# A diffusion block with two token mixers on one core: scan state carried by four 128x64 matmuls, inversion list in 64x64 tiles, order tables set anew

## The chip, the cores and the metric

The kernel runs on one core of a Trainium2 chip. The metric is the device time of one execution in microseconds (us). Five engines each work through a fixed list of instructions: TensorE (PE, its weight loads shown apart as PEld), VectorE (DVE), ScalarE (ACT), GpSimd (POOL) and SyncE (SP, which issues most of the DMA transfers). Each waits, through semaphores, for what the others produce.

## The reference

One layer is computed for 256 latent tokens, with 256 context tokens ahead of them as a prefix, all in fp32, with a width of 2048. Cut to what matters here:

```python
mod = silu(c) @ w_ada + b_ada                     # six shifts, scales and gates; the context has its own
h, hc = modulate(rmsnorm(x), ...), modulate(rmsnorm(ctx), ...)
rw, cv, z, ab, gt = split(h @ w_in)               # one projection feeds both mixers; gt are the merge gates
# mixer A, RWKV-7: 16 heads of 64, two directions, context first, then latent
s = s * w_t - (s @ kk_t) b_t + v_t k_t            # state, token by token;  y_t = s @ r_t
# mixer B, gated DeltaNet: 8 heads of 128, two directions, chunks of 64 tokens
u, wk = solve(I + strict_lower(kb kc^T * decay), [v*beta, kb*exp(gc)])
v_new = u - wk @ s;  o = q_dec @ s + qk @ v_new;  s = s * g_last + k_tail^T @ v_new
y = (sigmoid(g_a) * (o_a @ p_a) + sigmoid(g_b) * (o_b @ p_b)) @ w_out
x = x + gt1 * y
x = x + gt2 * swiglu(modulate(rmsnorm(x), ...))   # hidden width 5632
return rmsnorm(x, final_norm_w)
```

## The kernel before

**The products.** Each fp32 weight is split into a high and a low part (`whi` by an ACT cast, `wlo` by a DVE subtraction), the features likewise (`hxh`, `hxl`). A product is then three matmuls for each of the 16 k tiles: whi with hxh, whi with hxl, wlo with hxh. Matmuls between plain fp32 operands, which the mixers use, go to the chip as two instruction pairs (a weight load and a matmul each), so that one such matmul in the code is two matmul records in the trace and four instructions.

**Stages.** The modulation and the low-rank projections come first, up to about 200 us. Then comes the part that the change touches, which we call the weave, up to about 1310 us. It works through the RWKV heads in 8 pairs and then through the 8 DeltaNet heads. After it come the product with `p_a` (the pa stage, L377 to L379 for the matmuls, L362 to L368 for loading and splitting the weights), the product with `p_b`, `w_out`, the two halves of the feed-forward part, and the last norm.

**The weave.** Each piece of work (a pair's features, its Gram matrices, its inversion, its values, its scan; a head's features, Gram matrices, inversion, scan) is a Python generator that yields operations and waits. A planner (`Weave`, L179, its loop at L235) runs all generators against a model of the engines and emits the operations on PE, DVE, ACT and POOL in the order in which the model starts them; SP's list follows from that. The trace therefore puts all of these operations down to the one line that records them, L146, and the tiles' names tell them apart: `mm` is the PSUM bank of a projection product, `pi` that of an inversion, `s` that of a scan step, `pa` that of other mixer work.

The model has three tables. `LAT` gives the delays that it assumes: `dma` from a transfer's end to its data being usable, `hop` from one engine to another, `turn` for PE changing the kind of matmul. `RANK` settles who goes first among operations that could start at the same time. `GATES_A` and `GATES_B` (L28) say how many of the 40 gate products (matmuls with 256 columns that nothing in the weave waits for) come free at which pair or head. The projection products of later pairs and heads, and these gate products, are what PE does while a mixer's own chain waits for another engine (`products()`, L1060). They read `hxh` and `hxl`. The pa stage's tiles (`oah`, `oal`, `gts`, `PA`) lie in the space of `hxh` and `hxl`, so they can be written only after the last of these products has read it.

**The inversion** (`invert`, L563). The triangular 64x64 blocks of a pair (nu = 16) or of a head (nu = 8) are inverted in steps. Diagonal blocks of 16 rows are inverted on DVE after a round through DRAM, then pairs of blocks are joined: 16 to 32 to 64. The step from 16 to 32 is two lists of small matmuls with a DVE operation between them, and a copy and a transpose behind. The second list (L627) takes, for every block u, half h and quarter b, a 32x32 block of `Tx` as weights and 16 columns of `Qm`. Outside the 32x32 diagonal blocks `Tx` holds zeros at that point, because the DRAM scratch that it is read from was zeroed.

**The RWKV scan** (`scan`, L930). Each pair goes through eight steps: n = 0 to 3 over the context, 4 to 7 over the latent tokens. A step makes up to four lists of matmuls: the product of the state `vx` with `LAc` or `LAl` into a bank `ps`; from n = 1 to 6 the carry of the state into a second bank `acc`, done as a product with a block of the identity (`ident`, in the constants `C`; L967 to L969); from n = 4 the output's part of `LAl` by `vx`, into `acc`; and, after ACT has copied `ps` into `vx`, the lists with `KB` and `Pm`, which wait for that copy. DVE then scales `acc` into the next step's state.

Of the kernel before, what the change touches and what calls it, by code (L numbers as in the profile page):

```python
# [18 lines left out]
P = 128  # L19
# [5 lines left out]
NPAIR = 8  # L25
NGH = 8
DECAY = 0.6065306597126334
GATES_A, GATES_B = (6, 2, 1, 4, 0, 1, 4, 3), (2, 3, 0, 0, 2, 2, 9, 1)  # L28

RANK = dict(cast=-94, lowrank=-64, prepare=53, grams=-6, inverse=-58, values=6, scan=-54, begin=181, head_scan=90, head_inverse=115, head_grams=123, decays=122, tokens=90, features=160, gate_out=137, lowrank_out=99, row_tile=486)  # L30
LAT = dict(dma=2.4, hop=0.300, own=0.092, grp=32, cg=4, turn=0.170)
LNEXP = "natural_log_exp_and_others"
SIGM = "sigmoid_and_others"
UNIT = 64 * 64 + 64
# [66 lines left out]

HOP = LAT['hop']

# [174 lines left out]
def emit(ctx: ExitStack, tc, A, out, dbg=None):  # L278
# [6 lines left out]
    e, v, s = Lane(E, 0.0, 0.0, 0.0), Lane(V, 0.07, 0.00104, LAT["own"], 0.13), Lane(S, 0.09, 0.00086, LAT["own"], 0.165)  # L285
# [277 lines left out]
    def invert(pool, Lt, parts, nu, which, full, fill):  # L563
# [60 lines left out]
        for d in range(2):  # L624
            yield v.scalar_tensor_tensor(Qm[:, us[d]], pv[:, 0, us[d]], low16[:, d:d + 1],
                                         eye16[:, d].unsqueeze(1).to_broadcast([P, h2, 16]), ALU.mult, ALU.add)
        yield [e.matmul(pv[r, 1, u], Tx[r, u, b:b + 32], Qm[r, u, :], start=True, stop=True) for h, u, b, r in fours]  # L627
        for h in range(2):
            yield [(s.copy if h else v.tensor_copy)(T0[r, us[d], b + 16 * d:b + 16 * d + 16], pv[r, 1, us[d]])
                   for d in range(2) for b in (0, 32) for r in (slice(64 * h + b, 64 * h + b + 32),)]  # L630
# [59 lines left out]
    def c3(t):  # L690
        return t.rearrange("p (c t) -> p c t", t=64)
# [238 lines left out]
    def scan(p):  # L930

        o = pr[p]
        yield "values", p
        if p:
            yield "scan", p - 1

        VX = []
        for i, g0 in enumerate((2, 0)):
            vx = rs.tile([P, 8, 2, 64], F32, tag=f"VX{i}", name="VX")
            yield from turn(o["v"], g0, 2, lambda j, i, w: s.copy(  # L940
                vx.rearrange("p (d c) s k -> p d c s k", d=2)[half[1 - j], :, i::2, j, :],
                w.unsqueeze(1).to_broadcast([64, 2, 2, 64])))
            VX.append(vx)
        weave.ready("turned", p)
        yield "inverse", p
        for d in range(2):
            yield "grams", p, d
        LAl, LAc, KB, Pm, et = [o["la", d] for d in range(2)], [o["lc", d] for d in range(2)], o["KB"], o["Pm"], o["et"]
        Y = rs.tile([P, 4, 64], F32, tag="Y", name="Y")
        for n in range(8):  # L950
            m = n % 4
            vx, la = (VX[0], LAc) if n < 4 else (VX[1], LAl)
            cm = (m, 3 - m)
            cs_ = tuple(c + 4 * (n < 4) for c in cm)
            both = slice(m, 8 - m, 7 - 2 * m)
            dh = [(d, j, h) for d in range(2) for j, h in enumerate(half)]
            ps = yield psb
            ops = []
            for d, j, h in dh:
                w = slice(0, P) if n else half[1 - j]  # L960
                ops.append(e.matmul(ps[h, 64 * d:64 * d + 64], la[d][w, cm[d], j, 0:64], vx[w, 4 * d + cm[d], j, :],
                                    start=True, stop=True))
            yield ops

            acc = yield psb
            ops = []
            if 0 < n < 7:  # L967
                for j, h in enumerate(half):
                    ops.append(e.matmul(c3(acc[h, 0:P]), ident[h, h], vx[h, both, j, :], start=True, stop=False))  # L969
            if n >= 4:  # L970
                for d, j, h in dh:
                    ops.append(e.matmul(acc[h, P + 64 * d:P + 64 * d + 64], vx[:, 4 * d + cm[d], j, :],
                                        la[d][:, cm[d], j, 64:P], start=n == 7 and d == 0, stop=False))
            if ops:
                yield ops
            for j, h in enumerate(half):
                yield s.copy(vx[h, both, j, :], c3(ps[h, 0:P]))
            weave.release(psb)
            ops = []
            if n < 7:  # L980
                for d, j, h in dh:
                    ops.append(e.matmul(acc[h, 64 * d:64 * d + 64], KB[:, d, cs_[d], j, :], vx[:, 4 * d + cm[d], j, :],
                                        start=n == 0 and d == 0, stop=n < 4 and d == 1))
            if n >= 4:
                for d, j, h in dh:
                    ops.append(e.matmul(acc[h, P + 64 * d:P + 64 * d + 64], vx[h, 4 * d + cm[d], j, :], Pm[h, d, cm[d], :],
                                        start=False, stop=d == 1))
            yield ops
            if n < 7:
                c0 = cs_[0]  # L990
                end = et[:, c0:9 + cs_[1]:8 + cs_[1] - c0].unsqueeze(2)
                i = (n + 1) % 4
                vx = VX[0] if n < 3 else VX[1]
                for j, h in enumerate(half):
                    yield v.tensor_mul(vx[h, i:8 - i:7 - 2 * i, j, :], c3(acc[h, 0:P]), end[h].to_broadcast([64, 2, 64]))
            if n >= 4:
                y = Y[:, m:4 - m:3 - 2 * m] if m < 2 else Y[:, m::3 - 2 * m] if m == 3 else Y[:, 2:0:-1]
                if n < 6:
                    yield v.tensor_copy(y, c3(acc[:, P:2 * P]))
                else:  # L1000
                    yield v.tensor_add(y, c3(acc[:, P:2 * P]), y)
            weave.release(psb)
        weave.ready("scan", p)

        Yf = Y.rearrange("p c t -> p (c t)")
        g2 = rs.tile([P, P], F32, tag="gate", name="g2")[:64]
        Q.dma_start(g2, A["g2"][:, P * p:P * p + P])
        ps = yield pab
        yield e.matmul(ps[:, T:], g2, sgd, start=True, stop=True)
        gate = rs.tile([P, T], F32, tag="y3", name="gate")  # L1010
        yield s.copy(gate, ps[:, T:])
        yield e.matmul(ps[:, :T], bd64, Yf, start=True, stop=True)
        yield v.scalar_tensor_tensor(Yf, ps[:, :T], -1.0 / 64, Yf, ALU.mult, ALU.add)
        y2 = rs.tile([P, T], F32, tag="y2", name="y2")
        yield s.activation(y2, Yf, AF.Square)
        yield e.matmul(ps[:, :T], bd64, y2, start=True, stop=True)
        yield s.activation(y2, ps[:, :T], AF.Ln, bias=gneps, scale=1.0 / 64)
        weave.release(pab)
        yield s.activation(y2, y2, AF.Exp, scale=-0.5)
        yield v.tensor_mul(Yf, Yf, y2)  # L1020
        yield v.tensor_scalar(Yf, Yf, p_("lnw", p), p_("lnb", p), ALU.mult, ALU.add)
        yield v.tensor_add(Yf, Yf, o["kb"])
        yield v.tensor_mul(Yf, Yf, gate)
        Q.dma_start(oad[p], Yf)
        weave.ready("out", p)
        if dbg is not None:
            Q.dma_start(dbg["oa"][:, p, :], Yf)
# [735 lines left out]
```

## Time and profile before

| what | us |
| --- | --- |
| median of 3 runs | 2296.57 |
| lowest and highest of them | 2294.37 and 2297.48 |
| the profiled execution, whole | 2294.87 |
| the span of its trace | 2292.4 |

The mean clock that was granted to TensorE in that execution was 0.984 of full speed. The rows below are from the first page of the profile: the span in 40 equal slices of 57.3 us each. A digit is the busy share of a slice in tenths, the last row is what the DMA engines moved.

```profile
PE   7998999999999999999999989899999999999998
DVE  3446588888887587989888768774556665444444
ACT  3245554544455545554444455443444444444443
PEclk9999999999999999999999999999999999999999
DMA  9956543433443355556557796855777776566665
GB/s 383 406 149 171 174 114 105 108 102 98 108 103 102 96 167 141 162 160 172 173 169 229 248 351 224 283 187 165 231 232 234 232 231 212 187 183 186 185 188 161
```

The weave is slices 4 to 23. In slice 24, at 1310 us and after, the pa stage begins, and there the DMA moves 351 GB/s.

### The profile page before, as it was taken

The numbers are of one execution on the slowest core, as the hardware profiler recorded it, in microseconds if no ns is written. First come the engines' busy times: TensorE is split into PE (matmuls) and PEld (weight loads), VectorE is DVE, ScalarE is ACT, GpSimd is POOL, SyncE is SP. The second block draws the span as 40 slices with busy tenths as digits, with TensorE's granted clock in tenths as the row PEclk, the third lists the DMA queues.
The fourth block names the chain that finished last, engine by engine and source line by source line (L and its number), as shares of the span: only waits on it lengthen the run. The fifth ranks groups of instructions, "written<-read, shape, count | busy, mean of one in ns | idle before, by whom it ended". The sixth has DMA issues, their size and how long they took to land.

```text
span 2292.4 us, 55178 instructions
## 1 busy us (share of the span) xinstructions
PE 2189.3 (96%) x23160; PEld 1934.4 (84%) x23160; DVE 1570.3 (68%) x3233; ACT 1065.8 (46%) x1891; POOL 116.4 (5%) x185
## 2 busy tenths in 40 slices
PE   7998999999999999999999989899999999999998
PEld 4766587777777778888888879899999999999997
DVE  3446588888887587989888768774556665444444
ACT  3245554544455545554444455443444444444443
POOL 0000000000000010110110140000000000000000
PEclk9999999999999999999999999999999999999999
DMA  9956543433443355556557796855777776566665
GB/s 383 406 149 171 174 114 105 108 102 98 108 103 102 96 167 141 162 160 172 173 169 229 248 351 224 283 187 165 231 232 234 232 231 212 187 183 186 185 188 161
DMA packets 231928, 430.79 MB, mean 188 GB/s; under 512 B 114944, under 2 KB 129152, under 8 KB 227328
## 3 DMA queue, kind: packets, MB, share of 16 engines
q1 hardware_dynamic: 203744, 350.72, 49.4%
q0 software_dynamic: 14112, 51.39, 7.0%
q10 hardware_dynamic: 13824, 25.17, 3.3%
q8 instruction: 181, 2.97, 0.5%
q14 instruction: 67, 0.55, 0.1%
HBM read 401.44 MB, written 25.77 MB: 186 GB/s over the span
## 4 chain that ended last, share of the span: by engine, by line
PE 72%; DVE 11%; DMA 7%; issue 5%; ACT 4%; SPq 1%; POOL 0%; ACTq 0%; DVEq 0%; POOLq 0%
PE mm L146 19%; PE mm L377 13%; PE mm L379 12%; PE mm L378 12%; PE s L146 6%; PE pa L146 5%; DVE arena L146 3%; DVE wlo L146 2%; PE pi L146 2%; DMA wr<-wgu 1%; PE mm L465 1%; DVE aw L146 1%; DMA wraw<-pa 1%; DMA aw<-ada_rest 1%; DVE wlo L368 1%
## 5 line engine op out<-in xcount | busy, mean ns | idle before, releaser
L368 DVE TENSOR_TENSOR wlo<-wraw,whi 128x1024 fp32r<-128x1024 f32 x328 | 394.5, 1203 | 340.2 <-ACT whi L367 336.1
L367 ACT CAST whi<-wraw 128x1024 fp32r<-128x1024 f32 x328 | 338.2, 1031 | 484.7 <-PE mm L378 438.6
L146 PE MATMUL mm<-hxh,whi 128*128 128x256 f32 (+1 forms) x1376 | 465.9, 339 | 7.5 <-ACT whi L146 7.5
L146 PE MATMUL mm<-hxh,wlo 128*128 128x256 f32 (+1 forms) x1376 | 465.7, 338 | 5.5 <-DVE wlo L146 5.3
L146 PE MATMUL mm<-hxl,whi 128*128 128x256 f32 (+1 forms) x1376 | 466.1, 339 | 0.0
L377 PE MATMUL mm<-hfh,whi 128*128 128x256 f32 x1344 | 377.4, 281 | 0.0
L378 PE MATMUL mm<-hfl,whi 128*128 128x256 f32 x1344 | 376.3, 280 | 0.0
L379 PE MATMUL mm<-hfh,wlo 128*128 128x256 f32 x1344 | 374.2, 278 | 0.6 <-DVE wlo L368 0.6
L146 PEld LDWEIGHTS mm<-hxh,whi 128*128 128x128 f32 x1376 | 263.8, 192 | 35.6 <-ACT whi L146 8.5
L146 PEld LDWEIGHTS mm<-hxh,wlo 128*128 128x128 f32 x1376 | 263.6, 192 | 35.1 <-DVE wlo L146 7.6
L146 PEld LDWEIGHTS mm<-hxl,whi 128*128 128x128 f32 x1376 | 263.7, 192 | 27.3 <-issue 6.6
L146 DVE TENSOR_TENSOR wlo<-wraw,whi 128x512 fp32r<-128x512 f32 x344 | 235.9, 689 | 58.4 <-ACT whi L146 57.7
L146 ACT CAST whi<-wraw 128x512 fp32r<-128x512 f32 x344 | 206.8, 617 | 108.0 <-PE mm L146 75.2
L379 PEld LDWEIGHTS mm<-hfh,wlo 128*128 128x128 f32 x1344 | 252.8, 188 | 1.0 <-DVE wlo L368 1.0
L378 PEld LDWEIGHTS mm<-hfl,whi 128*128 128x128 f32 x1344 | 252.8, 188 | 0.0
L377 PEld LDWEIGHTS mm<-hfh,whi 128*128 128x128 f32 x1344 | 252.5, 188 | 0.0
L146 DVE TENSOR_TENSOR arena<-arena 128x28 f32<-128x28 f32 (+13 forms) x538 | 131.3, 247 | 22.7 <-DMA arena<-scr 8.0
L377 PE MATMUL mm<-za,whi 128*128 128x256 f32 x512 | 144.0, 281 | 0.0
L378 PE MATMUL mm<-za,whi 128*128 128x256 f32 x512 | 143.3, 280 | 0.0
L379 PE MATMUL mm<-za,wlo 128*128 128x256 f32 x512 | 142.4, 278 | 0.0
L146 DVE SCALAR_TENSOR_TENSOR aw<-aw,ck 128x512 f32<-128x512 f32 x120 | 90.0, 759 | 10.6 <-DMA aw<-ada_rest 10.4
L378 PEld LDWEIGHTS mm<-za,whi 128*128 128x128 f32 x512 | 96.3, 188 | 0.0
(320 smaller groups left out, 3939.2 us busy)
## 6 DMA issues: line engine op xcount, KB each, us to landing
wraw<-w SPq DMA_DIRECT2D x172, 512.0 KB, 4.1
wraw<-wgu SPq DMA_DIRECT2D x168, 512.0 KB, 4.6
aw<-ada_rest POOLq DMA_DIRECT2D x96, 512.0 KB, 5.3
aw<-ada_first SPq DMA_DIRECT2D x32, 1024.0 KB, 12.0
wraw<-wdn SPq DMA_DIRECT2D x64, 448.0 KB, 3.5
wraw<-wout SPq DMA_DIRECT2D x32, 512.0 KB, 4.8
aw<-ada_gt ACTq DMA_DIRECT2D x64, 256.0 KB, 5.1
wraw<-wdn SPq DMA_DIRECT2D x32, 512.0 KB, 3.6
```

What stands on the lines that cost most here:

```text
L146: return Op(self, cost, lambda: getattr(self.engine, name)(out, *a, **k), kind)
L367: S.copy(hi[:, c, :M], raw[:, c, :M])
L368: V.tensor_sub(lo[:, c, :M], raw[:, c, :M], hi[:, c, :M].bitcast(F32))
L377: E.matmul(ps, hi, Xh[:, k, :n], start=first and i == 0, stop=False)
L378: E.matmul(ps, hi, Xl[:, k, :n], start=False, stop=False)
L379: E.matmul(ps, lo, Xh[:, k, :n], start=False, stop=last and i == len(wt) - 1)
L465: E.matmul(ps[32 * g:32 * g + 32, 0:P], ckr[:, k].rearrange("p a b -> p (a b)"), aws[e, c][:, i, g], start=k == 0, stop=k == KT - 1)
```

## The change

There are three edits.

The second list of the inversion's step from 16 to 32 takes the whole 64x64 half of `Tx` as weights, for every block u and half h. The added weights are the zero blocks, so the result is the same. There are half as many matmuls: 32 instead of 64 for a pair, 16 instead of 32 for a head, with twice the weight columns each.

The carry of the scan's state uses the 128x64 half of the identity and 64 columns of the whole `vx` for each direction and half: four matmuls, where there were two with a 64x64 block of the identity and 128 columns.

The planner's tables change: one pair's and three heads' numbers of gate products (their sum stays 40), the rank of the heads' inversion, and the assumed delays `dma` and `hop`, each to 0.85 of what it was.

```diff
-GATES_A, GATES_B = (6, 2, 1, 4, 0, 1, 4, 3), (2, 3, 0, 0, 2, 2, 9, 1)
+GATES_A, GATES_B = (6, 2, 3, 4, 0, 1, 4, 3), (2, 3, 0, 1, 1, 0, 9, 1)
-RANK = dict(cast=-94, ..., head_scan=90, head_inverse=115, head_grams=123, ..., row_tile=486)
-LAT = dict(dma=2.4, hop=0.300, own=0.092, grp=32, cg=4, turn=0.170)
+RANK = dict(cast=-94, ..., head_scan=90, head_inverse=100, head_grams=123, ..., row_tile=486)
+LAT = dict(dma=2.04, hop=0.255, own=0.092, grp=32, cg=4, turn=0.17)
@@ invert
-        yield [e.matmul(pv[r, 1, u], Tx[r, u, b:b + 32], Qm[r, u, :], start=True, stop=True) for h, u, b, r in fours]
+        yield [e.matmul(pv[64 * h:64 * h + 64, 1, u], Tx[64 * h:64 * h + 64, u, :], Qm[64 * h:64 * h + 64, u, :],
+                        start=True, stop=True) for u in range(nu) for h in range(2)]
@@ scan
             if 0 < n < 7:
-                for j, h in enumerate(half):
-                    ops.append(e.matmul(c3(acc[h, 0:P]), ident[h, h], vx[h, both, j, :], start=True, stop=False))
+                for d, j, h in dh:
+                    ops.append(e.matmul(acc[h, 64 * d:64 * d + 64], ident[:, h], vx[:, 4 * d + cm[d], j, :],
+                                        start=d == 0, stop=False))
```

PE has 46,320 instructions before, 45,170 after: 1,536 fewer from the list, 384 more from the carry.

In the rows that follow, a name before the arrow is what is written, the names behind it what is read, then stand the result's rows by its columns and how many such matmuls follow each other. The first place is on PE, in a scan step from the fifth on (n = 4 to 6). Before:

```order
L146 MATMUL mm<-hxh,wlo 128x512
L146 MATMUL s<-VX,LAl 64x64 x4
L146 MATMUL s<-VX,C 64x128 x2
L146 MATMUL s<-LAl,VX 64x64 x4
L146 MATMUL mm<-hxh,whi 128x512
```

With the change:

```order
L146 MATMUL mm<-hxl,whi 128x512
L146 MATMUL s<-VX,LAl 64x64 x4
L146 MATMUL s<-VX,C 64x64 x4
L146 MATMUL s<-LAl,VX 64x64 x4
L146 MATMUL mm<-hxh,wlo 128x512
```

The three lists stand next to each other in both; only the one in the middle differs. The same holds for all 24 such steps.

The second place is on PE, between the two lists of a pair's step from 16 to 32 (`pi<-arena` is the first, `pi<-arena,Tx` the second; `pa` rows are work for the next pair). Before, in four of the eight pairs:

```order
L146 MATMUL mm<-hxh,wlo 128x512
L146 MATMUL pi<-arena 32x16 x64
L146 MATMUL pa<-LAl,arena 64x128 x16
L146 MATMUL mm<-hxh,whi 128x512
L146 MATMUL mm<-hxl,whi 128x512
L146 MATMUL mm<-hxh,wlo 128x512
L146 MATMUL pi<-arena,Tx 32x16 x64
L146 MATMUL mm<-hxh,whi 128x512
```

With the change, in one pair (in most of the others the same two kinds stand between the lists, with 6 to 8 projection matmuls):

```order
L146 MATMUL mm<-hxh,whi 128x512
L146 MATMUL pi<-arena 32x16 x64
L146 MATMUL pa<-C,arena 128x128 x2
L146 MATMUL mm<-hxl,whi 128x512
L146 MATMUL mm<-hxh,wlo 128x512
L146 MATMUL mm<-hxh,whi 128x512
L146 MATMUL mm<-hxl,whi 128x512
L146 MATMUL mm<-hxh,wlo 128x512
L146 MATMUL mm<-hxh,whi 128x512
L146 MATMUL pi<-arena,Tx 64x16 x32
L146 MATMUL pa<-LAc,arena 64x64 x16
```

The list of 16 `LAl` matmuls has moved from between the two lists, and more projection matmuls stand there; the second list is half as long.

The third place is on PE in the scan of the last DeltaNet head, in its third step (`s<-Qe,St`, `s<-PT,Vn`). Before:

```order
L146 MATMUL mm<-hxh,wlo 128x256
L146 MATMUL mm<-hxh,whi 128x256
L146 MATMUL s<-Qe,St 128x128
L146 MATMUL s<-PT,Vn 128x128
L146 MATMUL s<-Qe,St 128x128
L146 MATMUL s<-PT,Vn 128x128
L146 MATMUL mm<-hxl,whi 128x256
L146 MATMUL mm<-hxh,wlo 128x256
```

With the change:

```order
L379 MATMUL mm<-oah,wlo 128x256
L377 MATMUL mm<-oah,whi 128x256
L146 MATMUL s<-Vn,kta 128x128 x2
L146 MATMUL s<-Qe,St 128x128
L146 MATMUL s<-PT,Vn 128x128
L146 MATMUL s<-Qe,St 128x128
L146 MATMUL s<-PT,Vn 128x128
L378 MATMUL mm<-oal,whi 128x256
L379 MATMUL mm<-oah,wlo 128x256
L377 MATMUL mm<-oah,whi 128x256
```

What stands between the head's matmuls was gate products, and is now products of the pa stage: with the change the last gate product ends before the last head's inversion, and 211 matmuls of the pa stage stand between the pieces of its inversion and scan. Before, the pa stage's first matmul came behind all of them.

More of the change, by code (lines that the diff above doesn't have):

```diff
@@ L27 @@
 DECAY = 0.6065306597126334
-GATES_A, GATES_B = (6, 2, 1, 4, 0, 1, 4, 3), (2, 3, 0, 0, 2, 2, 9, 1)
-RANK = dict(cast=-94, lowrank=-64, prepare=53, grams=-6, inverse=-58, values=6, scan=-54, begin=181, head_scan=90, head_inverse=115, head_grams=123, decays=122, tokens=90, features=160, gate_out=137, lowrank_out=99, row_tile=486)
-LAT = dict(dma=2.4, hop=0.300, own=0.092, grp=32, cg=4, turn=0.170)
+GATES_A, GATES_B = (6, 2, 3, 4, 0, 1, 4, 3), (2, 3, 0, 1, 1, 0, 9, 1)
+RANK = dict(cast=-94, lowrank=-64, prepare=53, grams=-6, inverse=-58, values=6, scan=-54, begin=181, head_scan=90, head_inverse=100, head_grams=123, decays=122, tokens=90, features=160, gate_out=137, lowrank_out=99, row_tile=486)
+LAT = dict(dma=2.04, hop=0.255, own=0.092, grp=32, cg=4, turn=0.17)
 LNEXP = "natural_log_exp_and_others"
```

## The prediction

> **What bounds the kernel now.** I read the first page, then the windows of the weave, then PE's waits in it, then timelines at the places that the change touches.
>
> ```profile
> PE 2189.3 (96%) x23160; PEld 1934.4 (84%) x23160; DVE 1570.3 (68%) x3233; ACT 1065.8 (46%) x1891; POOL 116.4 (5%) x185
> q8 instruction: 181, 2.97, 0.5%
> 400.00:500.00 100.00, 96.06 (x1643) 75.36 (x1642) 83.47 (x206) 49.29 (x120) 4.52 (x10) 0.97 0.41 106
> 1000.00:1100.00 100.00, 97.56 (x973) 82.09 (x972) 91.94 (x240) 49.66 (x96) 10.36 (x16) 1.00 0.58 165
> ```
>
> PE is busy for 96% of the span, and for 96 and 98% in one stretch of the pairs (400 to 500 us) and one of the heads (1000 to 1100 us); the columns of a window are PE, PEld, DVE, ACT, POOL, the granted clock, the DMA share and GB/s. So inside the weave a matmul saved or added counts whole, whatever its chain waits for: other matmuls stand behind it. DVE is next, with 83 and 92 of 100 us.
>
> What PE waits for between 200 and 1310 us (total, times, longest, in us):
>
> ```profile
> PE pi L146 <- issue: 12.5, 8, 2.2
> PE s L146 <- DVE arena L146: 1.2, 6, 0.2
> PE pa L146 <- issue: 1.2, 2, 0.9
> PE s L146 <- ACT VX L146: 0.3, 1, 0.3
> ```
>
> The scan's hand-overs (VX, arena) cost next to nothing. The largest entry is no engine's result: 12.5 us in which an inversion matmul waits for nothing that the profile shows. The timeline of one pair shows where:
>
> ```profile
> 551.74 1.26 PE L146 MATMUL pi<-arena 32*32 32x16 f32 x128
> 552.93 0.99 PE L146 MATMUL pa<-LAl,arena 64*64 64x128 f32 x24
> 554.86 0.45 PE L146 MATMUL pa<-LAl,arena 64*64 64x128 f32 x8 [0.94 <-issue]
> ...
> 556.12 1.16 PE L146 MATMUL pi<-arena,Tx 32*32 32x16 f32 x117
> 559.14 0.37 PE L146 MATMUL pi<-arena,Tx 32*32 32x16 f32 x11 [1.86 <-issue]
> 559.45 0.80 PE L146 MATMUL mm<-hxh,whi 128*128 128x512 f32 x1
> 560.04 0.63 PE L146 MATMUL mm<-hxl,whi 128*128 128x512 f32 x1
> ```
>
> PE stops twice. Between the stops lie some 125 matmul records with a weight load each, about 250 instructions; and the page's q8 moved 2.97 MB in 181 packets for PE's 46,320 instructions and the others', 16.4 KB a packet, 256 instructions for PE alone (46,320 / 181). I take the stop for a block of instructions that was not there yet: the lists run at 9.3 ns a record (1.19 us / 128), so a block lasts 1.2 us there. Behind the second stop the next product's matmuls follow at 0.59 us (559.45 to 560.04) where the same form later takes 0.34 at most (below, 873.92 to 874.26): the clock was cut.
>
> ```profile
> 262.00:267.00 5.00, 5.00 (x15) 3.72 (x15) 2.33 (x5) 1.75 (x5) 0.00 (x0) 0.66 0.03 8
> 695.00:700.00 5.00, 5.00 (x89) 4.97 (x88) 4.15 (x9) 1.03 (x4) 0.00 (x0) 0.66 0.28 92
> 766.00:771.00 5.00, 5.00 (x143) 3.94 (x143) 4.76 (x9) 0.20 (x2) 0.00 (x0) 1.00 0.54 183
> ```
>
> Six of the eight pairs have such a window of 5 us at 0.66, of which these are the first and the last, and one of the two without. 0.66 over 5 us is a loss of 1.7 us of work, 10.2 us in all.
>
> **The inversion's list.** The trace has lists with weights of three widths; their times go from start to the next instruction's start.
>
> ```profile
> 873.27 0.73 PE L146 MATMUL pi<-arena,Tx 32*32 32x16 f32 x64
> 873.92 0.51 PE L146 MATMUL mm<-hxh,whi 128*128 128x512 f32 x1
> 874.26 0.39 PE L146 MATMUL mm<-hxl,whi 128*128 128x512 f32 x1
> ```
>
> That is a head's second list: 64 records of 32 weight columns take 0.65 us; a pair's, by the first list above, 1.19 for 128.
>
> ```profile
> 886.30 0.68 PE L146 MATMUL pi<-Tx,arena 64*64 64x64 f32 x16
> 886.91 0.51 PE L146 MATMUL mm<-hxh,wlo 128*128 128x512 f32 x1
> ```
>
> Sixteen records with 64 weight columns take 0.61 here, and eight (the scan's first list, below) 0.38: 0.15 to change the tile and 0.029 a record.
>
> ```profile
> 751.20 1.22 PE L146 MATMUL pa<-gtok,C 128*128 128x32 f32 x10
> 752.24 0.48 PE L146 MATMUL mm<-hxh,wlo 128*128 128x512 f32 x1
> ```
>
> Ten records with 128 weight columns and at most 64 moving ones take 1.04, or 0.104 each. Times the tiles in use at once (four, two, one) these are 37, 58 and 104 ns for 32, 64 and 128 weight columns, however many columns move. So I price the new list by its weights: a pair's 64 records take 0.15 + 64 x 0.029 = 2.0 us, 0.81 more than now; a head's 32 take 1.08, 0.43 more. Eight of each: **+9.9 us**. The other end is the number of records: the two lists now give 0.0084 us a record (0.54 / 64), and 64 and 32 fewer of them save 0.54 and 0.27, eight times: -6.5. I take the first, since its row has the form of the new list but for the columns moved. [...]
>
> **The scan's carry.** A step from n = 4 on:
>
> ```profile
> 530.73 0.45 PE L146 MATMUL s<-VX,LAl 128*64 128x64 f32 x8
> 531.11 0.44 PE L146 MATMUL s<-VX,C 64*64 64x128 f32 x4
> 531.48 0.45 PE L146 MATMUL s<-LAl,VX 128*64 128x64 f32 x8
> 531.86 0.50 PE L146 MATMUL mm<-hxh,whi 128*128 128x512 f32 x1
> ...
> 536.55 0.43 PE L146 MATMUL s<-VX,C 64*64 64x128 f32 x4 [0.20 <-DVE arena L146]
> ```
>
> The three lists take 1.13 us, because the one in the middle has another tile (64*64 between two of 128*64) and each change is paid. With the change all 24 records have the one tile: 0.15 + 24 x 0.029 = 0.85, so 0.28 less, for three steps of a pair. At n = 1 to 3 the pair of lists takes 0.38 + 0.37 now and 0.15 + 16 x 0.029 = 0.61 then: 0.14 less, three steps. That is 1.26 a pair and 10 in all. Some steps wait for DVE there anyway (0.20 in the last row), so I take **-8**, with ends of -10 and 0 (no tile change saved: 8 records of 0.38 for 4 of 0.37).
>
> **Blocks of instructions.** The lists of a pair now make 256 + 64 + 6 + 256 = 582 instructions within some 5 us; with the change, in most pairs 256 + 8 + 14 + 128, about 400, over a longer time, since more long matmuls stand between them and the second list runs at 29 ns a record. A block then lasts longer than its load in the second list (128 records x 29 ns = 3.7 us against 1.2). The first list is as dense as before. Of 13.7 us (12.5 + 1.2) I take half away and a little: **-8**, ends -14 and 0. [...]
>
> **The clock.** The cuts come behind the dense lists and their stops. If half of the pairs lose them, 10.2 us become 5: **-5**, ends -10 and +3 (all eight pairs cut).
>
> **The end of the weave.**
>
> ```profile
> 1310.00:1320.00 10.00, 7.21 (x45) 6.71 (x46) 6.43 (x13) 4.15 (x11) 2.00 (x3) 0.83 0.96 329
> 1320.00:1330.00 10.00, 7.40 (x55) 6.45 (x53) 5.96 (x5) 6.93 (x12) 6.14 (x7) 1.00 1.08 388
> 1330.00:1340.00 10.00, 4.89 (x25) 4.58 (x24) 2.99 (x3) 2.27 (x4) 2.67 (x3) 0.70 1.00 401
> 1340.00:1350.00 10.00, 9.54 (x67) 9.28 (x66) 8.12 (x7) 4.76 (x7) 3.24 (x5) 0.79 0.83 275
> ```
>
> And what waited there, a transfer's issue and one of the matmuls:
>
> ```profile
> 1310.39 0.93 POOL L1553 DMA_DIRECT2D gts<-gts__1351  x1 [22.00 <-PE mm L146]
> 1339.47 0.58 PE L377 MATMUL mm<-oah,whi 128*128 128x256 f32 x1 [4.36 <-ACT whi L367]
> ```
>
> Here PE is idle for 2.8 + 2.6 + 5.1 + 0.5 = 11 us, and the clock of 0.83, 0.70 and 0.79 costs up to 1.7 + 3.0 + 2.1 = 6.8 more: 18 us, while the DMA moves 329 to 401 GB/s. PE waits for weights (the last row) that share the DMA with the gates' transfers, and these could start only when the last product had read the features (the POOL row: 22 us of waiting for `mm`). With the change that last product ends before head 7's inversion, so the transfers begin while PE still has that head's inversion and scan to do, some 13 us of its own matmuls by my count of them at the durations above, and the pa stage's first 211 matmuls fill the gaps between. The DMA's work is the same; it only starts earlier. I take **-11**, ends -18 and 0 (the head's chain waits on DVE and ACT as long as the filler lacks weights).
>
> **Shorter delays in the tables.** `hop` and `dma` set no wait on the chip; they put instructions earlier in PE's list than before. Where the result isn't there yet, PE stops, and everything behind it on PE with it. There are some 190 round trips through another engine in the scans (8 pairs x 8 steps x 2, and 8 x 8 of the heads), each drawn 2 x 0.045 us closer: 17 us if every one of them is short by all of it. And 48 transfers in the inversions (three for each of 16), each drawn 0.36 us closer: 17 more.
>
> ```profile
> arena<-sgd__1342 SPq DMA_DIRECT2D x32, 256.0 KB, 3.4
> ```
>
> The inversions' transfers landed 3.4 us after their issue, which the old table's 2.4 plus the transfer (0.7 for 256 KB at the 360 KB/us that the planner assumes) does not quite cover either; yet PE's waits for them are small. A chain that comes late pushes only its own list, as the 0.3 and 1.2 us on VX and arena show. I take **+5**, ends 0 and +34.
>
> **The sum**: 9.9 - 8 - 8 - 5 - 11 + 5 = -17.1. From the profiled execution's 2294.87 that is 2277.8; the median lies 1.7 above that execution, so the forecast is **2279 us**.
>
> **Rivals.** (B) *The end of the weave gains nothing*: the DMA is already at 329 to 401 GB/s there, and if earlier transfers only fight with the 256-column products' weights, the sum is -6 and the time 2290.5. For it: those four windows. Against it: the weave's own DMA share of 0.41 and 0.58 leaves room. (C) *The list follows its matmuls, not its weights*: 16.4 less, so 2262.5. For it: no row has few columns moved with 64 weight columns. Against it: the ten records at 0.104. (D) *The stops and the cuts of the clock stay*: 13 more, so 2292. For it: the first list is unchanged, and its 256 instructions are a block on their own. Against it: the longer stop of the pair above lies in the second list. (E) *The order is drawn for a chip with faster hand-overs than this one*: PE's list puts scan lists and inversion lists ahead of products that could have run, and pays for it at each, up to 34. At full price 29 above the forecast: 2308, slower than before. It decides once more than 17 of the 34 us reach PE. For it: 3.4 us to land against less assumed; DVE at 92% in the heads, so that its results come late. Against it: the four rows of waits.
>
> **How the numbers follow.** The forecast has 0.54; B 0.12; C 0.10; D 0.12; E 0.12. The forecast's own range, with two of its terms at their ends, is 2268 to 2291. The 80% range is 2262 to 2296: it takes in B and D, reaches to C, and leaves out most of E and the forecast's far ends. A measurement of this kernel tells a difference of about 0.2%, 4.6 us, from none. Faster: 0.52 of the forecast, C, 0.07 of B, 0.05 of D: 0.74. Same: the rest of the forecast, of B and of D, 0.14. Slower: E, 0.12.
>
> **What would show it.** A pair's second list should take 2.0 us from start to the next instruction, a head's 1.08; 1.3 and 0.6 or less would be C. The carry should read x8 with tile 128*64, and the three lists 0.85. The inversions' issue waits should total 6 us or less, and three or four of the pairs show a 5 us window at 0.66; 12 and six are D. In the 40 us behind the last feature product PE should be idle for less than 4 us; 11 is B. PE's waits for VX, arena and transfers should stay under 10 us; 20 or more is E. The forecast is wrong altogether if DVE, not PE, becomes the engine that others wait for in the heads.

## The result and the profile after

The changed kernel's median is 2288.12 us (20 executions, 2279.46 to 2295.60), that of the kernel before 2294.49 us (20, 2286.64 to 2297.83). The ratio is 0.9974 with a 95% interval of 0.9961 to 0.9986: 6 us faster, where 17 were forecast. The profiled execution took 2291.02 us, its span is 2289.2 us at a mean granted clock of 0.978, so it is one of the slower ones.

From the first page of the changed kernel:

```profile
PE 2191.2 (96%) x22584; PEld 1944.7 (85%) x22584; DVE 1566.3 (68%) x3233; ACT 1068.0 (47%) x1894; POOL 115.2 (5%) x185
q8 instruction: 177, 2.90, 0.5%
```

What PE waits for between 200 and 1310 us (total, times, longest):

```profile
PE s L146 <- DVE VX L146: 3.5, 5, 1.9
PE pa L146 <- DVE LAc L146: 2.9, 1, 2.9
PE pi L146 <- issue: 2.0, 1, 2.0
PE pa L146 <- issue: 0.9, 1, 0.9
PE s L146 <- DVE arena L146: 0.8, 4, 0.2
```

The rows are a choice from the view. The issue waits are down from 13.7 to 2.9 us. New are waits on DVE: 3.5 us for the scan's state and 2.9 for one LAc. All of PE's waits on ACT, DVE and the DMA between 200 and 1260 us add up to 27.4 us in the kernel before and 30.1 in the changed one.

The lists that the change edits, in the timeline of the changed kernel, each with the instruction behind it:

```profile
351.26 2.04 PE L146 MATMUL pi<-arena,Tx 64*64 64x16 f32 x64 [0.28 <-DVE arena L146]
353.23 0.50 PE L146 MATMUL mm<-hxh,wlo 128*128 128x512 f32 x1
...
534.22 0.45 PE L146 MATMUL s<-VX,LAl 128*64 128x64 f32 x8
534.50 0.40 PE L146 MATMUL s<-VX,C 128*64 128x64 f32 x8
534.73 0.41 PE L146 MATMUL s<-LAl,VX 128*64 128x64 f32 x8
535.07 0.38 PE L146 MATMUL mm<-hxh,wlo 128*128 128x256 f32 x1
...
897.53 1.11 PE L146 MATMUL pi<-arena,Tx 64*64 64x16 f32 x32
898.57 1.16 PE L146 MATMUL pa<-arena 128*128 128x128 f32 x8
```

A pair's second list takes 1.97 us (353.23 - 351.26; 2.0 was forecast), a head's 1.04 (1.08), a step's three lists 0.85 (0.85).

Now the stretch around the end of the weave, in windows of 90 us (us, then PE, PEld, DVE, ACT, POOL, granted clock, DMA share, GB/s). The kernel before:

```profile
1260.00:1350.00 90.00, 78.86 (x820) 74.25 (x820) 59.32 (x101) 41.16 (x82) 18.30 (x25) 0.92 0.83 285
1350.00:1440.00 90.00, 85.84 (x715) 83.33 (x713) 74.77 (x104) 50.72 (x76) 18.65 (x22) 1.00 0.79 266
```

The changed kernel, the same two windows and four of 10 us within them:

```profile
1260.00:1350.00 90.00, 82.44 (x843) 77.82 (x843) 58.92 (x135) 46.12 (x87) 16.34 (x21) 0.98 0.76 249
1350.00:1440.00 90.00, 79.30 (x638) 76.16 (x637) 76.86 (x105) 43.46 (x68) 21.80 (x26) 0.96 0.83 284
...
1310.00:1320.00 10.00, 9.55 (x92) 9.28 (x91) 2.90 (x7) 7.09 (x14) 3.45 (x4) 1.00 1.07 399
1330.00:1340.00 10.00, 10.00 (x85) 10.00 (x85) 3.83 (x7) 4.04 (x8) 2.68 (x2) 0.95 0.44 139
1370.00:1380.00 10.00, 5.98 (x41) 4.80 (x39) 8.19 (x12) 4.68 (x7) 4.68 (x4) 0.94 0.84 297
1380.00:1390.00 10.00, 8.44 (x56) 8.45 (x57) 8.97 (x13) 2.51 (x3) 1.58 (x3) 0.72 0.93 352
```

As a measure of what PE loses there I take its idle time plus the clock's shortfall times the window. Before: 11.1 + 4.2 idle and 0.08 x 90 = 7.2 of clock, 22.5 us. After: 7.6 + 10.7 idle, 1.8 + 3.6 of clock, 23.7 us. The first window lost less, the second more by as much: PE is busy and the DMA full at 1310 us, PE is busy and the DMA at 139 GB/s at 1330, and at 1370 to 1390 PE stops, with the DMA at 297 to 352. The largest of PE's waits between 1340 and 1440 us there is for the low parts of the weights, which DVE makes:

```profile
PE mm L379 <- DVE wlo L368: 6.7, 6, 3.5
```

### The profile page after: what moved, and what is told of

It is laid out like the page before. It is cut to its first block, busy times and chain, and to the rows that moved or that the text cites. A ratio compares the mean times of both kernels' runs of the same rounds, so it can differ in the third digit from the quotient of the medians.

```text
span 2289.2 us, 53997 instructions
## 1 busy us (share of the span) xinstructions
PE 2191.2 (96%) x22584; PEld 1944.7 (85%) x22584; DVE 1566.3 (68%) x3233; ACT 1068.0 (47%) x1894; POOL 115.2 (5%) x185
## 5 line engine op out<-in xcount | busy, mean ns | idle before, releaser
L379 PEld LDWEIGHTS mm<-za,wlo 128*128 128x128 f32 x512 | 96.4, 188 | 0.0
```

Source lines behind the costliest of these rows:

```text
L379: E.matmul(ps, lo, Xh[:, k, :n], start=False, stop=last and i == len(wt) - 1)
```

## The experiments

Times of the kernel before differ between chips and hours by some us (its medians in the six sets of runs are 2289.19 to 2294.49), so each run is given by its ratio to executions of the kernel before on the same chip, and in us as (ratio - 1) x 2291. "New order" is the list of instructions that the new tables give, "old order" that of the kernel before. To change a matmul without moving anything else in the weave, its operations were wrapped so that the planner saw the other form's count, cost and kind:

```diff
+dress = lambda ops, like: [Op(ops[0].lane, c, lambda p=ops[i * len(ops) // len(like):(i + 1) * len(ops) // len(like)]: [o.call() for o in p], k) for i, (c, k) in enumerate(like)]
```

### The three edits apart: e1 to e4, e10, e11

In the new order, the old list (e2), the old carry (e10) and both (e1):

```diff
-        yield [e.matmul(pv[64 * h:64 * h + 64, 1, u], Tx[64 * h:64 * h + 64, u, :], ...) for u in range(nu) for h in range(2)]
+        yield dress([e.matmul(pv[r, 1, u], Tx[r, u, b:b + 32], Qm[r, u, :], ...) for h, u, b, r in fours], [(0.022, (64, 64))] * (2 * nu))
...
-                for d, j, h in dh: ops.append(e.matmul(acc[h, 64 * d:64 * d + 64], ident[:, h], ...))
+                for j, h in enumerate(half): ops.append(e.matmul(c3(acc[h, 0:P]), ident[h, h], ...))
+                ops = dress(ops, [(0.058, (P, 64))] * 4)
```

In the old order the same the other way round: the new list (e3), the new carry (e11), both (e4).

> The new order in the weave, with the old list (32x32 tiles) and the old carry in the same places. Theory L (the new list is what costs: 10 us of matmul time and the longer cuts of the clock; the order is what gains): faster than the kernel before by 10 to 16 us, 2279 to 2285, mean clock of its runs 0.983 or more, no cut longer than 3.4 us behind the pairs' lists. Theory O (the new order's own waits on PE, such as 2.9 us for LAc, bring the cuts of 10 us): clock 0.981 or less in the mean, cuts of 10 us still there, and 0 to 6 us faster. Issue waits of the inversions: 5 to 13 us, since the old list's 256 instructions are back.

> The changed kernel with only the second list put back to 32x32 tiles, everything else in its place. Theory L: 10 us of list time and some 6 us of clock are saved, 5 to 10 us of issue waits come back: 2276 to 2283, clock 0.983 or more. Theory O: the clock stays at 0.981, the list's 10 us and the issue waits nearly cancel: 2285 to 2290.

> The kernel before with only the second list in 64x64 tiles, everything else in its place. Theory L: list 10 us more, issue waits 8 us less, the clock down to 0.981 or less (6 us): 2297 to 2305. Theory O: the clock stays where the kernel before has it, 2293 to 2298. In both a pair's list takes 1.97 us at full clock and a head's 1.04.

> The kernel before with both edits of the matmuls (64x64 list, four 128x64 carries) in the old places. By the forecast's terms the carry takes 8 us off whatever e3 shows: theory L 2289 to 2297, theory O 2285 to 2290. If it stands within 3 us of e3, the carry's saving is not on the path.

> The changed kernel with the old carry (two 64x64 matmuls with 128 columns), everything else in its place. The steps' lists measured 57.5 us in the kernel before and 52.0 in the changed one: 5.5 to 8 us slower than the changed kernel, 2292 to 2295. Theory C2 (the carry saves more in the new order, since there the steps are closer together): 10 to 13 us slower, 2296 to 2300, as e2 against e1.

> The kernel before with the new carry alone, in the old places: 5.5 to 8 us faster than the kernel before by the steps' measured times (2283 to 2286); by theory C2 only 2 to 4 us (2287 to 2290).

| order, list, carry | run | ratio (95%) | us |
| --- | --- | --- | --- |
| new, old, old | e1 | 1.0005 (0.9982 to 1.0029) | +1 |
| new, old, new | e2 | 0.9944 (0.9921 to 0.9966) | -13 |
| old, new, old | e3 | 1.0022 (1.0004 to 1.0040) | +5 |
| old, new, new | e4 | 0.9993 (0.9976 to 1.0009) | -2 |
| new, new, old | e10 | 1.0012 (0.9993 to 1.0031) | +3 |
| old, old, new | e11 | 0.9972 (0.9955 to 0.9989) | -6 |
| new, new, new | changed | 0.9974 (0.9961 to 0.9986) | -6 |

One of the seven has another order than its row says. Ahead of the last matmul of the last head's scan stand 211 matmuls of the pa stage in the changed kernel, e2 and e10, and none in the four of the old order; in e1 there are 259, at other places between the pieces of the last head. So e1 differs at the end of the weave too, and its pairs are not read as the price of one edit.

That leaves three pairs for each edit. The list: +5 (e3), +5 (e4 to e11), +7 (changed to e2), 5.5 in the mean. The carry: -6 (e11), -7 (e4 to e3), -9 (changed to e10), -7. The order: -2 (e10 to e3), -6 (e2 to e11), -4 (changed to e4), -4. By the table's intervals a single difference is uncertain by 5 to 6 us, and the three of an edit share runs. For the order the forecast's terms were -8 for the blocks, -5 for the clock, -11 for the end and +5 for the delays, -19, of which part of the -8 belongs to the list: the order's part is the one that is missing.

Against each its expectations: e1 came out slower than either theory had it; e2 as theory L; e3 as L in its time, near its lower end; e11 and e10 show the carry at about the forecast's size in the old and the new order, so theory C2 falls.

How the list and the order share the issue waits is seen in PE's waits from 200 to 1310 us of e11 (old order, old list):

```profile
PE pi L146 <- issue: 13.8, 9, 2.2
```

of e3 (old order, new list):

```profile
PE pi L146 <- issue: 8.1, 6, 1.8
```

and of e2 (new order, old list):

```profile
PE pi L146 <- issue: 4.5, 3, 2.2
...
PE pa L146 <- issue: 2.7, 3, 1.2
```

With the waits of the `pa` rows, the list takes them from 13.7 us (kernel before) to 9.7 (e3), the order from 14.8 (e11) to 7.3 (e2), and both together leave 2.9.

### The clock: e8

The changed kernel again.

> The changed kernel itself, for its clock beside the kernel before on one chip. Theory L (the new list draws longer cuts of the clock): mean clock 0.002 or more below that of the kernel before, 5 us. Theory N (the cuts differ from execution to execution and the two profiles were a good and a bad draw): the two mean clocks agree within 0.001, and the ratio is 0.997 again.

The ratio is 0.9978 (0.9958 to 0.9997), again 5 us. The mean clock of its 12 executions is 0.982, that of the 20 of the changed kernel 0.981, and that of 131 executions of the kernel before 0.981: theory N. What a single profile shows can be seen from three windows at pairs' inversions, in the changed kernel's first profile:

```profile
423.00:433.00 10.00, 10.00 (x183) 8.24 (x175) 4.21 (x11) 5.18 (x15) 0.00 (x0) 0.50 0.11 30
491.00:501.00 10.00, 10.00 (x92) 8.62 (x89) 6.14 (x17) 0.68 (x2) 0.00 (x0) 0.52 0.19 58
573.00:583.00 10.00, 10.00 (x111) 8.30 (x110) 6.00 (x14) 4.16 (x11) 0.00 (x0) 0.51 0.32 102
```

and in the second, the same windows (by the third, its instructions lie 10 us earlier; its mean clock is 0.99 from 400 to 600 us and 1.00 from 600 to 800):

```profile
423.00:433.00 10.00, 10.00 (x243) 8.05 (x243) 5.98 (x14) 6.84 (x18) 0.00 (x0) 0.83 0.18 52
491.00:501.00 10.00, 10.00 (x211) 8.70 (x209) 9.22 (x19) 6.58 (x17) 0.00 (x0) 1.00 0.29 99
573.00:583.00 10.00, 9.42 (x196) 8.30 (x188) 9.72 (x20) 5.48 (x14) 1.46 (x4) 1.00 0.11 28
```

Three cuts of 10 us in one, a single one of 3.4 us at half clock (0.17 x 10 x 2) in the other; the spans are 2289.2 and 2277.3 us. The means of some other kernels do differ from the 0.981 of the kernel before: 0.985 in e7 and e18 (12 executions), the fastest, and 0.977 in e9 and e16 (20), the slowest. So a part of their times may lie in the clock, which no run here separates.

### The end of the weave: e5, e6, e7, e18, e9, e13, e14

First, what came late there. In the changed kernel POOL could issue the loads of the second modulation (`aw<-ada_rest`, L1528), which began at 1311 us before the change, only from 1340 us on, 3 us before the last matmul of the last head's scan starts (in e8 and e5 it is 3 us too; before the change it was 3 us behind that matmul):

```profile
1340.27 1.65 POOL L1528 DMA_DIRECT2D aw<-ada_rest  x3
```

e5 (changed kernel), e6 (kernel before) and e7 with e18 (as e2) move 13 of the 16 loads that lie in the pa stage to the pb stage:

```diff
@@ pa stage
-        next(scale_next)
+        if j > 12: next(scale_next)
@@ pb stage
-        if j > 12:
+        if j >= 0:
             next(scale_next)
```

> The changed kernel with 13 of the 16 loads of the second modulation (aw<-ada_rest, 512 KB each, with their DVE accumulations) taken out of the pa stage and spread over the pb stage. Theory G (the end of the weave gave its gain back because these loads, which began at 1311 us before the change, now cannot begin before the last head has left its space, 1340 us, and crowd the rest of the pa stage): PE's idle time between 1340 and 1400 us falls from about 14 us to under 6, and the kernel comes out 5 to 10 us faster than the changed kernel, 2277 to 2283. Theory H (the last head's own hand-overs to DVE cost what was gained): idle there stays over 12 us, time unchanged, 2286 to 2290.

> The kernel before with the same 13 loads moved. Theory G: before the change these loads lie beside the gates' transfers and the first pa weights at 1311 to 1340 us, only a few of them in the 30 us that stop PE; the gain is smaller than in e5, 2 to 5 us of the 18 lost there: 2286 to 2292. Theory H: the same small gain in both kernels.

> The new order and carry with the old 32x32 list, and the 13 loads moved: theory G 2270 to 2276 (e2 less 4 to 8), theory H 2277 to 2281, as e2. If it holds, it beats both kernels.

> e7 once more (6 runs there): 2274 to 2280, clear of the changed kernel's 2287; if the moved loads bring nothing, as e2, 2278 to 2282.

e5: 0.9953 (0.9930 to 0.9975), 11 us faster than the kernel before and so 5 faster than the changed kernel, as theory G had it. In the window that the expectation names, 1340 to 1400 us, PE is idle for 3.9 us in e5, against 8.7 and 7.5 in the two profiles of the changed kernel; the 14 that the fall was to start from were not there. e6: 0.9998 (0.9978 to 1.0018), nothing. e7 and e18: 0.9924 (0.9895 to 0.9954) and 0.9919 (0.9891 to 0.9947), 17 and 19 us faster than the kernel before, 5 faster than e2.

Taken one by one these 5 us lie within the intervals, so the traces have to say where they come from. The first matmul of the pa stage and the first of `w_out`, in the kernel before:

```profile
1311.58 0.51 PE L377 MATMUL mm<-oah,whi 128*128 128x256 f32 x2 [1.60 <-ACT oah L382]
...
1422.40 0.28 PE L377 MATMUL mm<-mh,whi 128*128 128x256 f32 x1
```

in the changed kernel:

```profile
1300.42 0.50 PE L377 MATMUL mm<-oah,whi 128*128 128x256 f32 x2 [1.32 <-ACT oah L382]
...
1423.23 0.28 PE L377 MATMUL mm<-mh,whi 128*128 128x256 f32 x1
```

and in e5:

```profile
1295.07 0.50 PE L377 MATMUL mm<-oah,whi 128*128 128x256 f32 x2 [1.32 <-ACT oah L382]
...
1410.70 0.36 PE L377 MATMUL mm<-mh,whi 128*128 128x256 f32 x1 [0.29 <-DVE arena L1580]
```

From one to the other it is 110.8, 122.8 and 115.6 us. The changed kernel's second profile has 121.2 and e2 122.6; e7 and e18, with the loads moved, have 117.2 and 117.5; e6, in the old order, has 112.5. So in the new order the late loads cost 4 to 7 us of this stretch and in the old one none.

Second, the old end in the new order: ten gate products held back to the last head.

```diff
-GATES_A, GATES_B = (6, 2, 3, 4, 0, 1, 4, 3), (2, 3, 0, 1, 1, 0, 9, 1)
+GATES_A, GATES_B = (6, 2, 3, 4, 0, 1, 4, 3), (2, 3, 0, 1, 1, 0, 0, 10)
```

> The changed kernel with the last ten gate products held back to the last head (GATES_B ending in 0, 10 for 9, 1). PE's order is the same up to the seventh head; behind that the gate products fill the last head's scan again and the pa stage's first matmul comes after it, as before the change. Theory B (the early start of the pa stage is worth nothing, since the DMA is then idle where PE works on the last head's chain and PE is idle where the DMA is full): within 3 us of the changed kernel, 2284 to 2290. The forecast's term (-11 for the early start): 2294 to 2300.

e9: 1.0049 (1.0031 to 1.0067), 11 us slower than the kernel before. Its windows show that this is no price of the end alone:

```profile
1200.00:1260.00 60.00, 45.06 (x479) 38.42 (x478) 46.10 (x140) 23.20 (x48) 5.92 (x10) 0.80 0.58 176
1260.00:1350.00 90.00, 82.35 (x837) 78.22 (x836) 60.29 (x122) 40.49 (x85) 13.98 (x20) 0.96 0.78 260
1350.00:1440.00 90.00, 84.00 (x687) 81.92 (x688) 75.38 (x100) 50.89 (x78) 19.11 (x24) 0.96 0.78 271
```

The end loses 7.7 + 6.0 idle and 3.6 + 3.6 of clock, 21 us, a little less than in any of the others; but the seventh head, which lacks the products now, loses 14.9 + 12 us between 1200 and 1260, where the changed kernel loses 1.2. The expectation could not be told by the time; by the windows it is theory B.

Third, seven of the eight gate transfers left out, in the kernel before (e13) and the changed one (e14):

```diff
-    gts = gp.tile([P, 32, T], F32, name="gts")
-    for i in range(0, 32, 4):
+    gts = gp.tile([P, 4, T], F32, name="gts")
+    for i in range(0, 4, 4):
...
-        G.tensor_mul(PA[:, j], PA[:, j], gts[:, j])
+        G.tensor_mul(PA[:, j], PA[:, j], gts[:, j % 4])
```

> The kernel before with one of the eight transfers of the merge gates (gts, 512 KB each) in place of eight: all channels use the first four rows of gates. It takes 3.7 MB out of the stretch behind the weave, 9 to 10 us at the 380 GB/s seen there. Forecast's picture (PE stops there for weights that share the DMA with the gates): 8 to 12 us faster than the kernel before, 2279 to 2284, PE's idle time between 1260 and 1440 us down from 15 to 6 or less.

> The changed kernel with the same seven transfers left out. Theory T0 (the stretch is as full as before, the early start only moved it): 8 to 12 us faster than the changed kernel, as in e13, 2275 to 2279. Theory T1 (the changed order hides these transfers): within 3 us of the changed kernel, 2284 to 2290, and idle time between 1260 and 1440 us as before, 16 to 21.

e13: 0.9999 (0.9983 to 1.0016), no gain; e14: 0.9957 (0.9942 to 0.9971), 4 to 5 us faster than the changed kernel, between its two theories (and with 283 pa matmuls ahead of the last head's end instead of 211, so not quite in the same order). In e13 the pa stage runs as forecast, and stops at its end:

```profile
1340.00:1350.00 10.00, 9.84 (x81) 9.42 (x79) 7.96 (x7) 5.83 (x10) 2.13 (x4) 1.00 1.01 379
1360.00:1370.00 10.00, 5.15 (x23) 3.83 (x23) 9.34 (x10) 3.33 (x5) 9.98 (x14) 0.70 0.35 109
```

With the gates' transfers gone PE is at 98% while the DMA moves 379 GB/s, and in the 40 us behind the last feature product it is idle for 4.4 us instead of 11.0: that part of the forecast's picture holds. The stop at 1360 is partly the experiment's own: the one small tile of gates lets no multiplication by gates begin before the last sigmoid, so all 16 fall together on POOL, and DVE's splits with them (last section). e13 and e14 therefore don't settle whether the gates' transfers are hidden; they show that what is gained in the pa stage can be lost at its end.

### The shorter delays: e12, e17, e15

```diff
-LAT = dict(dma=2.04, hop=0.255, own=0.092, grp=32, cg=4, turn=0.17)
+LAT = dict(dma=2.4, hop=0.300, own=0.092, grp=32, cg=4, turn=0.170)
```

in the changed kernel (e12, e17), and the reverse in the kernel before (e15).

> The changed kernel with the assumed delays dma and hop put back (2.4 and 0.300), the other tables and the matmuls as changed; PE's order moves again. The forecast's term (+5 for delays that are too short): 2280 to 2284, with less than 25 us of PE waits on ACT, DVE and DMA between 200 and 1260 us (30 in the changed kernel). Theory W (the shorter delays cost nothing, since the order they give also has fewer issue waits): 2285 to 2292.

> e12 once more (6 runs there, and its profiled one the slowest but for none): if the delays' price of 8 us is real, 2276 to 2281 again; if e12 was a good draw, 2284 to 2288 as the changed kernel.

> The kernel before with the two shorter delays (dma 2.04, hop 0.255) alone; PE's order moves. If e12 shows the price of the delays, this is 5 to 10 us slower than the kernel before: 2296 to 2302, with over 30 us of PE waits on ACT, DVE and DMA between 200 and 1260 us. If the price belongs to the pair of that table with the other tables (theory P: each set of numbers gives an order of its own, and none of them has a price by itself), anything from 2284 to 2296.

e12 and e17: 0.9940 (0.9918 to 0.9961) and 0.9950 (0.9934 to 0.9967), 14 and 11 us faster than the kernel before, 6 to 8 faster than the changed kernel, e12 a little below its range. e15: 1.0021 (1.0006 to 1.0035), 5 us slower than the kernel before. So the shorter delays cost 5 to 8 us with either set of the other numbers. The waits that were to show it did not come out as expected: all of PE's waits on ACT, DVE and the DMA between 200 and 1260 us are 26.3 us in e12 and 28.0 in e17 (under 25 was expected), 29.0 in e15 (over 30), with 30.1 and 32.3 in the two profiles of the changed kernel and 27.4 in the kernel before. Each setting also gives a whole order of its own, so the price is that of the orders drawn with these delays.

### What looked best put together: e16

The changed kernel with the old delays, the old list (its own cost, so that the order moves) and the moved loads.

> What the runs so far favour: the new gate numbers, rank and carry, with the old delays, the old 32x32 list and 13 loads of the second modulation moved to the pb stage. If the savings add up (e12 -8, the old list -5, the moved loads -3, from the changed kernel's 2287): 2269 to 2274. Theory P: 2274 to 2284.

1.0024 (1.0011 to 1.0038), 5 us slower than the kernel before, outside both expectations. In this order 379 matmuls of the pa stage stand before the last head's end, where the changed kernel has 211:

```profile
1260.00:1350.00 90.00, 74.73 (x795) 71.74 (x794) 52.42 (x122) 38.95 (x76) 17.09 (x17) 0.87 0.66 217
1350.00:1440.00 90.00, 81.00 (x630) 76.46 (x628) 73.93 (x115) 46.18 (x71) 20.21 (x28) 0.95 0.83 283
```

15.3 + 9.0 us idle, 11.7 + 4.5 of clock: 40.5 us lost at the end. The fastest kernel of the study stays e7 (e18), the new order and carry with the old list and the moved loads.

## Why the prediction was wrong, by its own steps

**What bounds the kernel.** PE, as said: 96% busy before and after, and the savings on PE in the weave show in the time in either order.

**The list.** Right: 1.97 and 1.04 us, by the number of weight columns, +9.4 us on PE's list where +9.9 was forecast. Rival C is out. The whole kernel shows +5.5, since the list takes 4 to 6 us of issue waits with it (13.7 to 9.7 in the old order, 7.3 to 2.9 in the new). The rows of 64 and 128 weight columns carried the step, and the run bears them out with 16 columns moving, which no row had: (1.97 - 1.04) / 32 = 0.029 us a record, the price that the prediction took from rows with 64 moving.

**The carry.** Right in its mechanism and size: no change of tile, 0.85 for 1.13. Three pairs of kernels give -7, the forecast -8; in the profiles all the steps' lists with their waits go from 57.4 to 51.9 us.

**Blocks of instructions.** Right, and larger than taken: 13.7 us became 2.9, -10.8 for -8. That the stops belong to blocks of 256 instructions fits the trace: from stop to stop the kernel before has 2,032 recorded instructions of PE (1,016 matmuls and as many weight loads) in five of seven cases, eight blocks less 16, and 256 in the case shown in the prediction. Rival D is out as far as the stops go.

**The clock.** The step "if half of the pairs lose them, 10.2 us become 5" failed. The mean clock is 0.981 before and after; in one profile the changed kernel had three cuts three times as long, in another almost none. The cuts differ from execution to execution, and the term was read from one. By the means it is 0.

**The end of the weave.** This is the step that failed most: "The DMA's work is the same; it only starts earlier. I take -11, ends -18 and 0." Its beginning came true. The last feature product ended at 1299 us instead of 1310 (behind the first lists of the last head's inversion, and not before all of it), the transfers started earlier, and in the 40 us behind that product PE was idle for 4.5 us, 3.3 in e8, where it had been 11.0; under 4 was the sign that the prediction named. But the gain was given back in what followed, which the sign did not cover. Of the 122.8 and 121.2 us from the first pa matmul to the first of `w_out`, some 11.5 are what was left of the last head's own matmuls (from start to next start, waits left out; 13.7 as PE's busy time, 13 by the forecast's count). That leaves 108 to 111 us for the pa and pb stages, which took 110.8 before: in this stretch the early start was worth 0 to 3 us, not 11. By idle time and clock in the two windows of 90 us nothing was gained either: 22.5 us before, 23.7 and 28 in the two profiles of the changed kernel.

The pa products were put where gate products had been, and these were used up before. While PE worked on the last head, the DMA fell to 139 GB/s: the loads that had run at 1311 us came only at 1340 (that they wait for the last head's space is read from the code and from the moment, which goes with the last head's end in each profile). Then they stood beside the rest of the weights, DVE had their accumulations on top, and PE stopped at 1370 to 1390, most of it for DVE's low parts, instead of at 1310 to 1340. Moving 13 of them on takes 4 to 7 us out of this stretch in the new order (e5, e7, e18) and none in the old (e6), which shows this cause for about half of what was missing. For the rest, the used-up filler is argued and not shown: e9, which holds it back, loses less at the end and 27 us in the seventh head, but the loss in the two windows does not simply grow with the pa matmuls ahead of the last head's end. It is 21 to 24 us with none (e13 and e14, which lack the gates, left out), 24 to 32 with 211 and the loads in their old place, 22 to 26 with 211 and the loads moved, 25 to 28 with 98 (e15), 259 (e1) and 283 (e12, e17), and 40.5 with 379 (e16).

Rival B, "the end of the weave gains nothing", is what happened to this term, though not by its sign (11 us of idle time in those 40 us). It had 0.12. That its sum of -6 is also the measured change is luck in part, since it kept the 5 us of the clock that did not come.

**Shorter delays.** Right in sign and about in size: 5 to 8 us by e12, e17 and e15 for the +5 taken. Rival E's full 34 is out. Its sign was badly set: PE's waits for VX, arena and transfers between 200 and 1310 us were to stay under 10 us, but were 12 in the kernel before already, as the four rows that the prediction shows leave out larger ones (4.9 us for ACT's arena, 3.2 for transfers); they are 18 in the changed kernel.

**The sum.** The forecast's terms without the clock's 5 and the end's 11 are -1. What the runs give for the edits, +5.5 for the list with its issue waits, -7 for the carry and -4 for the order, makes the measured -6, as differences along the same runs must. Between -1 and -6 lies what single profiles can't settle: two of one kernel differ by 12 us. The forecast's own range of 2268 to 2291, "with two of its terms at their ends", does not say which two; the widest give 2266 and, without the delays' 34, 2298.

## What to carry to other kernels

A fixed stock of filler work covers waits only once: before crediting a new order with a stall removed, name what fills the place from which the filler was taken, and what the transfers that start earlier have to wait for next. Let the sign reach as far as the work that was moved: here PE's idle time fell in the first 40 us and came back in the 60 behind them. Price edits of matmuls by the nearest forms' start-to-start times, which held to 4% here; price stalls and cuts of the clock from several executions, since one profile gave a sign that 20 executions did not. Savings found apart in an order drawn by a planner need not add up (e16), and a run shows the price of one edit alone only where its order is the same to the end, which e1's is not.

## What the runs showed of the hardware that was not expected

In the profiles of the two kernels every cut of the clock is to 0.50, and of those that end within the trace, 17 in each, one lasts about 3.4, 6.8 or 10.2 us (14, 3 and none in the kernel before; 9, 5 and 3 in the changed one). With the same instructions at the same place the cuts lasted 10 us in one execution and 3.4 or none in another (the six windows under e8). PE reads busy for all 10 us of the longest ones; what sets a cut off, and what ends it, no run here tests.

While POOL multiplied by the gates, one of DVE's subtractions of two tiles took 5.25 us in place of 0.61. In the timeline of e13, on DVE:

```profile
1358.95 5.32 DVE L383 TENSOR_TENSOR oal<-arena,oah 128x256 fp32r<-128x256 f32 x6
...
1364.53 0.61 DVE L383 TENSOR_TENSOR oal<-arena,oah 128x256 fp32r<-128x256 f32 x1
1365.95 5.25 DVE L383 TENSOR_TENSOR oal<-arena,oah 128x256 fp32r<-128x256 f32 x1
```

and on POOL:

```profile
1356.90 7.96 POOL L1576 TENSOR_TENSOR PA<-PA,gts 128x256 f32<-128x256 f32 x8 [1.79 <-ACT gts L1559]
...
1365.42 5.50 POOL L1576 TENSOR_TENSOR PA<-PA,gts 128x256 f32<-128x256 f32 x8
```

The last subtraction stood for as long as eight multiplications ran, and PE waited 4.85 us for it; six others, beside the eight multiplications before, took 0.89 each. Why the last one took as long as all eight and these did not stays unexplained.
